# Two decoder layers on one core: u, Toeplitz blocks and halves of q and k moved by transfers instead of part-height ScalarE copies, with a new instruction order and first weights in two parts

## Chip, core and metric

The kernel runs on 1 core of one Trainium2 chip, as one launch. The metric is device microseconds of that core for one execution; smaller is better. Before and after are timed as medians of runs.

## What is computed

Two layers over 512 tokens of width 1024, in float32:

```
for l in range(2):
    h = x @ w_in[l]                       # 1024 -> q | k | v | u, 512 columns each
    attn = diff_attention(q, k, v, ...)   # 4 heads, two score maps of 64 dims each, rotary on q and k, causal
    ssm  = s5_ssm(u, ...)                 # 32 groups of 16 channels, a complex state of 64 each; GELU, GLU (512 x 512)
    mix  = concat(attn, ssm) @ w_out[l]
    x = layer_norm(ALPHA * x + mix)
    x = layer_norm(ALPHA * x + square(relu(x @ w_ff1[l])) @ w_ff2[l])   # 1024 -> 4096 -> 1024
```

## The kernel before

**Products.** Each float32 product is three products of split operands (`mm3`): high x high, high x low, low x high. A weight of 128 x 1024 comes as `raw` by a transfer from SyncE's queue; ScalarE casts it to `whi`; the rest `wlo` is subtracted by VectorE or GpSimd (letters V and P in the plan), or written by ScalarE negated and then completed by an adding transfer that GpSimd issues (A).

**Stages of a layer.** First the "back": projections q, k, v, u of four tiles each, and among them four attention heads in four blocks of 128 tokens and the SSM in four quads (`ssm_pars`, `ssm_outp`, `ssm_a`, `ssm_b`, `ssm_c`), then the four GLU tiles g. Then the mix product with a layer norm, then the feed-forward in eight chunks with a layer norm. In layer 0 the back runs until about 200 us of the profile, in layer 1 from about 550 to 760 us.

**The order.** All instructions are recorded first (`Rec.add`), with a cost each (`Rec.cost`) and a distance between producer and consumer (`Rec.lat`). A list scheduler (`run`) then places them engine by engine, by rank plus an offset per group from the table `pri`, and writes them out in the order of its own clock. So every row of every engine, and SyncE's queue, stands in one planned order; each engine then works through its own rows strictly in turn. Where the planner sees TensorE idle for more than 500 ns, it puts in products of zeros (`wz`, 128 x 256) whose results nobody reads; they keep TensorE occupied. 18 of them stand at the start in any case. I call them fillers.

**Three places with part-height copies.** All of them move rows between partitions:
- `uproj`: a projected tile of u lies in PSUM as 128 channels x 512 tokens, and the SSM wants it as four blocks of 32 partitions by token residue: 16 ScalarE copies of 32 x 128 each, `u<-ps_acc`.
- `ssm_outp`: the Toeplitz block `mx` is filled from `m3` by one full copy and six copies of 32 x 128, `mx<-m`.
- `qkproj`: after the rotary step q is split into high and low, and the halves (64 partitions) are put above each other in two tiles `xq`. For q these are two casts and two subtractions of half height; for k four casts, two subtractions and two memsets of half height into four tiles. The rotary step itself swaps 32-row blocks with four transfers `rt<-rt`.

`cmul` puts its result into `gx` or `hx` with four half-height copies.

**Start.** `start` loads the first two weights (u0 and q0), each in one transfer of 512 KB, one cast and one subtraction of 1024 columns, between eight slices of x.

Of the kernel before, what the change touches and what calls it, by code (L numbers as in the profile page):

```python
# [13 lines left out]
F32 = mybir.dt.float32  # L14
# [32 lines left out]
    "att": [[8, 11, 14, 18], [8, 12, 15, 18]],  # L47
    "s5": [[4, 14], [3, 13]],
# [3 lines left out]
    "eng": {"rope": ["VVV", "VVV"], "tab": ["VVVVVV", "VVVVVV"], "cg": ["VVVV", "VVPV"], "ch": ["VVVV", "VVVV"], "sa": ["PV", "VP"], "sb": ["VVVVVV", "VVVVVV"]},  # L52
    "flo": "AVVV",
    "nlo": "APVAVPPV",
    "glo": "VPPPAPV",
    "seq": "f m1 m7 f m2 m4 f m6 f m5 m3",
    "elo": "VVVV",
    "wb": 4,
    "s5o": "p1 p0 o0 a0 b0 a1 c0 p2 o1 b1 a2 c1 b2 p3 a3 o2 b3 c2 o3 c3",
    "swq": "S",  # L60
    "ao": [-6000, 4000],
    "so": [2000, 19000],
    "ap": [40500, 56750],
    "sp": [31000, 27000],
# [3 lines left out]
    "cuts": [0, 8],  # L68
# [1600 lines left out]
```

## Time and profile before

| | before |
|---|---|
| time, median of 3 runs | 1150.72 us (1150.34 to 1151.69) |
| time of the profiled execution | 1151.48 us |
| its span, first to last instruction | 1149.7 us |
| TensorE busy | 1117.1 us (97%) |
| VectorE busy | 912.5 us (79%) |
| ScalarE busy | 632.2 us (55%) |
| GpSimd busy | 260.3 us (23%) |
| DMA packets | 154.12 MB, mean 134 GB/s |

TensorE's records overlap each other, so its busy share is high even where products start late; and its busy time holds the fillers. Stretches of the span have to be read one by one, since the back of a layer and the feed-forward load the engines differently.

### The profile page before, as it was taken

Reading aid. Unit: us, or ns where it says so; the run is one execution under the profiler, and the core shown is the slowest. Engines: PE = TensorE matmul, PEld = TensorE weight load, DVE = VectorE, ACT = ScalarE, POOL = GpSimd, SP = SyncE. Lnnn points to the kernel's source line nnn. Section 1 sums busy time; section 2 is a strip of 40 time slices with the busy share of each in tenths; the row PEclk is TensorE's granted clock in tenths of the full one; section 3 lists DMA queues with packets and bytes.
Section 4 is the critical chain, followed back from the end, with each engine's and each line's share of the span. In section 5 each row is a group of like instructions: output and inputs, shape, how many; then the busy total and the mean of one; then the engine's idle time right before and its main releaser. Section 6 shows DMA issues by size and latency. Waiting matters only on the chain.

```text
span 1149.7 us, 16190 instructions
## 1 busy us (share of the span) xinstructions
PE 1117.1 (97%) x5840; PEld 936.0 (81%) x5840; DVE 912.5 (79%) x1569; ACT 632.2 (55%) x1202; POOL 260.3 (23%) x198
## 2 busy tenths in 40 slices
PE   9999999999999999999999999999999999999997
PEld 7778877889888888888788878878988888888885
DVE  7898998887778878767792988867777778778788
ACT  7886869425544464444537788873454445445440
POOL 1011110311232242133021221022032143133221
PEclk9999999999999999999999999999999999999999
DMA  9443642441562452553678662652444454355231
GB/s 320 101 119 75 156 121 65 157 135 58 147 155 86 129 168 86 147 147 99 197 202 216 173 169 63 191 155 79 137 139 123 134 128 129 110 147 129 91 110 74
DMA packets 50960, 154.12 MB, mean 134 GB/s; under 512 B 6848, under 2 KB 7104, under 8 KB 50880
## 3 DMA queue, kind: packets, MB, share of 16 engines
q1 hardware_dynamic: 42240, 121.63, 32.6%
q0 software_dynamic: 8640, 31.46, 15.3%
q8 instruction: 46, 0.75, 0.3%
q14 instruction: 34, 0.28, 0.1%
HBM read 110.07 MB, written 7.34 MB: 102 GB/s over the span
## 4 chain that ended last, share of the span: by engine, by line
PE 66%; ACT 5%; DVE 2%; issue 2%; DMA 1%; SPq 0%; DVEq 0%; ACTq 0%; POOLq 0%
PE ps_acc L506 35%; PE ps_sc L506 23%; PE ps_s L506 8%; ACT whi L506 1%; ACT u L506 1%; DVE xq L506 1%; DVE wlo L506 1%; ACT at L506 1%; ACT wlo L506 1%; DMA wlo<-raw 0%; DMA keep<-xq 0%; ACT xq L506 0%; ACT xTh L506 0%; DVE xTl L506 0%; DMA xq<-xs 0%
## 5 line engine op out<-in xcount | busy, mean ns | idle before, releaser
L506 ACT CAST whi<-raw 128x1024 fp32r<-128x1024 f32 x222 | 232.2, 1051 | 264.2 <-PE ps_acc L506 129.4
L506 PE MATMUL ps_acc<-xTh,whi 128*128 128x512 f32 (+1 forms) x712 | 268.9, 379 | 4.6 <-ACT u L506 3.7
L506 PE MATMUL ps_acc<-xTl,whi 128*128 128x512 f32 (+1 forms) x712 | 268.3, 378 | 1.7 <-DVE xTl L506 1.3
L506 PE MATMUL ps_acc<-xTh,wlo 128*128 128x512 f32 (+1 forms) x712 | 268.0, 378 | 0.0
L506 PE MATMUL ps_sc<-whi,slot 128*128 128x512 f32 x784 | 254.5, 391 | 1.2 <-DVE xq L506 0.6
L506 POOL TENSOR_TENSOR wlo<-raw,whi 128x1024 fp32r<-128x1024 f32 x62 | 156.2, 2519 | 418.7 <-ACT whi L506 410.9
L506 PEld LDWEIGHTS ps_sc<-whi,slot 128*128 128x128 f32 x784 | 147.0, 188 | 34.6 <-issue 4.1
L506 DVE TENSOR_TENSOR wlo<-raw,whi 128x1024 fp32r<-128x1024 f32 x100 | 122.0, 1221 | 47.1 <-ACT whi L506 47.0
L506 PEld LDWEIGHTS ps_acc<-xTh,whi 128*128 128x128 f32 x712 | 134.0, 188 | 29.3 <-ACT u L506 4.5
L506 PEld LDWEIGHTS ps_acc<-xTl,whi 128*128 128x128 f32 x712 | 134.1, 188 | 24.7 <-DVE xTl L506 1.9
L506 PE MATMUL ps_sc<-wlo,slot 128*128 128x512 f32 x392 | 153.0, 390 | 0.0
L506 PEld LDWEIGHTS ps_acc<-xTh,wlo 128*128 128x128 f32 x712 | 133.9, 188 | 22.9 <-DMA wlo<-raw 0.3
L506 DVE TENSOR_TENSOR slot<-slot 128x512 fp32r<-128x512 f32 (+4 forms) x143 | 126.5, 893 | 6.5 <-ACT slot L506 6.0
L506 POOL DMA_DIRECT2D wlo<-raw x60 | 53.0, 887 | 231.5 <-ACT wlo L506 114.6
L506 ACT ACTIVATE wlo<-raw 128x1024 fp32r<-128x1024 f32 x60 | 63.4, 1059 | 61.9 <-PE ps_s L506 32.4
L506 PEld LDWEIGHTS ps_sc<-wlo,slot 128*128 128x128 f32 x392 | 73.6, 188 | 14.7
L506 DVE TENSOR_TENSOR xq<-xq,ps_sc 128x512 f32<-128x512 f32 x124 | 83.1, 679 | 0.7 <-PE ps_sc L506 0.7
L506 DVE TENSOR_TENSOR raw<-raw 128x1024 f32<-128x1024 f32 x56 | 68.4, 1221 | 0.6
L506 ACT CAST slot<-slot 128x512 fp32r<-128x512 f32 x56 | 34.5, 617 | 51.1 <-DVE slot L506 49.1
L506 PE MATMUL ps_acc<-whi,xTh 128*128 128x256 f32 (+1 forms) x176 | 56.4, 320 | 0.8 <-ACT u L506 0.7
L506 PE MATMUL ps_acc<-wlo,xTh 128*128 128x256 f32 (+1 forms) x176 | 55.9, 319 | 0.4 <-DVE wlo L506 0.4
L506 PE MATMUL ps_acc<-whi,xTl 128*128 128x256 f32 (+1 forms) x176 | 55.4, 318 | 0.0
(229 smaller groups left out, 1902.3 us busy)
## 6 DMA issues: line engine op xcount, KB each, us to landing
raw<-in_w_ff_dram SPq DMA_DIRECT2D x128, 512.0 KB, 3.5
wlo<-raw POOLq DMA_DIRECT2D x60, 512.0 KB, 5.3
raw<-in_w_qk_dram SPq DMA_DIRECT2D x16, 512.0 KB, 5.2
raw<-in_w_out_dram SPq DMA_DIRECT2D x16, 512.0 KB, 4.1
raw<-in_w_u_dram SPq DMA_DIRECT2D x8, 512.0 KB, 5.4
raw<-in_w_v_dram SPq DMA_DIRECT2D x8, 512.0 KB, 6.6
rt<-rt SPq DMA_DIRECT2D x64, 64.0 KB, 2.6
at<-in_ln_dram SPq DMA_DIRECT2D x16, 256.0 KB, 4.4
```

What stands on the lines that cost most here:

```text
L506: getattr(self.real[op.eng], op.name)(*[_real(x) for x in op.a], **{n: _real(x) for n, x in op.k.items()})
```

## The change

Nothing that is computed changes. What moves data changes in four places, and the order changes everywhere.

- `uproj` (`um` is D in both layers): one ScalarE copy of 128 x 512 from PSUM into a tile `rt`, one transfer of 256 KB to a DRAM tile `ud`, four transfers of 64 KB back into `u`.
- `ssm_outp` (`mm` is D): the six small copies become three transfers of 32, 64 and 96 partitions, `mx<-m3`; the layout of `mx` turns from `[P, 4, P]` to `[P, T, 4, 32]`.
- `qkproj` (`qm` is DD and DA): q in both layers and k in layer 0 are cast and subtracted once at full height; transfers of 64 x 512 then fill `xq`: four for a q, eight for a k. Layer 1's k stays as it was.
- `cmul`: two half-height copies in place of four.
- `start` with cuts 0, 2, 8: each of the first two weights comes as 256 and then 768 columns.
- Planner: part-height operations, accumulating ScalarE operations, float32 products, the products that read `xq`, transfers to fewer than 128 partitions, GpSimd copies and ScalarE's release of a buffer cost more; `att`, `s5`, `s5o`, offsets and `pri` (92 entries before, 117 now, 110 of these new or changed) are other numbers. Which engine makes `wlo` changes for 34 weights: 16 go from VectorE to ScalarE with the adding transfer, 18 from VectorE to GpSimd.

```diff
-    "att": [[8, 11, 14, 18], [8, 12, 15, 18]],
-    "s5": [[4, 14], [3, 13]],
+    "att": [[8, 11, 14, 20], [9, 10, 15, 18]],
+    "s5": [[4, 14], [3, 14]],
...
-    "flo": "AVVV",
+    "flo": "AVPP",
...
-    "glo": "VPPPAPV",
+    "glo": "AVPPAPV",
...
-    "cuts": [0, 8],
+    "cuts": [0, 2, 8],
...
+    "um": ["D", "D"],
+    "qm": ["DD", "DA"],
+    "mm": ["D", "D"],
+    "cc": ["AA", "AA", "AA", "AA"],
...
-            return (650.0 if o.p[1] - o.p[0] == 32 else 475.0) if e == "DMA" else 1030.0, 1550.0 + 1.35 * op.move
+            return (690.0 if o.p[1] - o.p[0] < 128 else 520.0) if e == "DMA" else 1030.0, 1550.0 + 1.35 * op.move
...
+            if r.dt == F32R and r.t.key[1] == "xq":
+                return max(c + {256: 35.0, 384: 50.0, 512: 42.0}.get(o.idx.size, 13.2), 116.0), 0.0
...
+            t += 113.0 * (o.p[1] - o.p[0] < P)
...
+            if PLAN["mm"][l] == "D":
+                Q.dma_start(out=mx[0:(t + 1) * 32, t].rearrange("p a c -> p (a c)"),
+                            in_=m3[(3 - t) * 32:128].rearrange("p a c -> p (a c)"))
+            else:
...
+        if PLAN["qm"][l][z] == "D":
+            A.copy(swp.bitcast(F32R), src)
+            tt(src, swp, SU, src.bitcast(F32R), PLAN["ql"][l][2 * h + z])
+            if z == 0:
+                ta, tb = slot(F32R, "xq"), slot(F32R, "xq")
+                for t_, p, o in ((ta, lo, hi), (tb, hi, lo)):
+                    Q.dma_start(out=t_[p].bitcast(F32), in_=swp[p])
+                    Q.dma_start(out=t_[o].bitcast(F32), in_=src[p])
+                qk_t[l, h, z] = ta, tb
+            else:
+
+                f = [slot(F32R, "xq") for i in range(4)]
+                for i, (w, p) in enumerate(((swp, lo), (swp, hi), (src, lo), (src, hi))):
+                    for o in (lo, hi):
+                        Q.dma_start(out=f[i][o].bitcast(F32), in_=w[p])
+                qk_t[l, h, z] = tuple(f)
...
+        if PLAN["um"][l] == "D":
+
+            w = v4(slot(tag="rt"))
+            A.copy(w, av)
+            d = dram.tile([P, 512], F32, name=f"ud{l}{ct}")
+            Q.dma_start(out=d, in_=w.rearrange("p t n -> p (t n)"))
             for t in range(T):
-                A.copy(u[t * 32:(t + 1) * 32, j, :], av[j * 32:(j + 1) * 32, t, :])
+                Q.dma_start(out=u[t * 32:(t + 1) * 32], in_=d[:, t * P:(t + 1) * P].blocks(4))
```

The order of rows is shown at three places. The first is ScalarE at the very start of the program, before:

```order
L506 CAST whi<-raw 128x1024
L506 CAST xTh<-slot 128x512
L506 CAST whi<-raw 128x1024
L506 CAST xTh<-slot 128x512 x2
L506 ACTIVATE mh<-sm 128x32
```

and now:

```order
L523 CAST whi<-raw 128x256
L523 CAST xTh<-slot 128x512
L523 CAST whi<-raw 128x256
L523 CAST xTh<-slot 128x512
L523 CAST whi<-raw 128x768
L523 CAST xTh<-slot 128x512
```

The casts of the first two weights stand in two pieces, and the second slice of x comes ahead of the larger pieces. In TensorE's rows 18 fillers stand ahead of the first product instead of 30.

The second place is ScalarE behind the second rotary projection of layer 0 (k0), where the first two tiles of u leave PSUM. Before:

```order
L506 ACTIVATE rt<-ps_acc 128x512
L506 ACTIVATE wlo<-raw 128x1024
L506 CAST whi<-raw 128x1024
L506 COPY u<-ps_acc 32x128 x16
L506 CAST xq<-rt 64x512 x2
L506 ACTIVATE wlo<-raw 128x1024
L506 COPY u<-ps_acc 32x128 x16
```

and now:

```order
L523 ACTIVATE rt<-ps_acc 128x512
L523 CAST whi<-raw 128x1024
L523 COPY rt<-ps_acc 128x512
L523 ACTIVATE wlo<-raw 128x1024
L523 CAST whi<-raw 128x1024
L523 CAST rt<-rt 128x512
L523 ACTIVATE wlo<-raw 128x1024
L523 CAST whi<-raw 128x1024
L523 CAST rt<-rt 128x512
L523 COPY rt<-ps_acc 128x512
```

Each row of 16 small copies is one full copy, and the second of these stands behind the casts of q0 and k0 (`CAST rt<-rt`), which wait for the rotary step and its transfers. TensorE's rows hold 53 fillers at this place, ahead of the product that needs the bank which the second copy frees; before, 12 stood a little later.

The third place is SyncE's queue in the same stretch and behind it. Before:

```order
L506 DMA rt<-rt 32x512 x4
L506 DMA raw<-in_w_u_dram 128x1024
L506 DMA dsk<-in_d_s_dram 128x32
L506 DMA gsub<-in_subln_dram 128x2
L506 DMA hb<-in_glu_b_dram 128x8
L506 DMA raw<-in_w_qk_dram 128x1024
L506 DMA raw<-in_w_v_dram 128x1024 x2
```

and now:

```order
L523 DMA xq<-rt 64x512 x8
L523 DMA ud_670<-rt 128x512
L523 DMA ud_675<-rt 128x512
L523 DMA raw<-in_w_qk_dram 128x1024
L523 DMA u<-ud_419 32x4x128 x4
L523 DMA raw<-in_w_v_dram 128x1024 x2
L523 DMA u<-ud_670 32x4x128 x4
L523 DMA u<-ud_675 32x4x128 x4
L523 DMA mx_98<-m_943 32x128
L523 DMA mx_98<-m_943 64x128
L523 DMA mx_98<-m_943 96x128
```

The weight transfers now stand between transfers that wait for computed tiles. SyncE's queue has 466 transfers in all instead of 336. In all of the program 117 fillers stand instead of 168; the products that compute are the same 5,368 before and now.

## Rows read from the trace of the kernel before

**Rows 1.** The page: busy time of each engine, share of the span, instructions.
```profile
PE 1117.1 (97%) x5840; PEld 936.0 (81%) x5840; DVE 912.5 (79%) x1569; ACT 632.2 (55%) x1202; POOL 260.3 (23%) x198
```

**Rows 2.** Windows: stretch, length, busy us (instructions) of PE, PEld, DVE, ACT, POOL.
```profile
25.00:200.00 175.00, 163.79 (x1037) 136.58 (x1037) 158.06 (x422) 136.00 (x363) 23.89 (x35) 0.99 0.43 110
200.00:550.00 350.00, 349.09 (x1659) 292.37 (x1659) 273.25 (x369) 164.63 (x232) 97.47 (x54) 1.00 0.45 127
550.00:760.00 210.00, 201.43 (x1254) 173.25 (x1253) 167.56 (x332) 151.01 (x363) 38.55 (x47) 1.00 0.63 172
760.00:1140.00 380.00, 378.12 (x1779) 314.66 (x1778) 289.65 (x379) 163.77 (x222) 95.62 (x53) 1.00 0.43 119
```

**Rows 3.** The same for the fillers' tile wz alone: PE busy first.
```profile
25.00:200.00 175.00, 15.37 (x127) 12.16 (x127) 0.00 (x0) 0.99 0.43 110
```

**Rows 4.** Waits of PE, 25 to 200 us: for whom, us, times, longest.
```profile
PE ps_s L506 <- ACT mx L506: 2.8, 2, 1.6
PE ps_acc L506 <- ACT u L506: 2.6, 3, 1.4
PE ps_sc L506 <- ACT xq L506: 0.8, 1, 0.8
```

**Rows 5.** Waits of PE, 550 to 760 us.
```profile
PE ps_s L506 <- ACT u L506: 2.0, 3, 1.4
PE ps_acc L506 <- ACT u L506: 1.9, 2, 1.6
```

**Rows 6.** Timeline of PE from 683 us: start, us, what [idle before].
```profile
683.49 0.28 PE L506 MATMUL ps_acc<-whi,xTh 128*128 128x256 f32 x1
685.37 0.50 PE L506 MATMUL ps_acc<-xTh,whi 128*128 128x512 f32 x1 [1.60 <-ACT u L506]
685.71 0.39 PE L506 MATMUL ps_acc<-xTl,whi 128*128 128x512 f32 x1
685.94 0.39 PE L506 MATMUL ps_acc<-xTh,wlo 128*128 128x512 f32 x1
```

**Rows 7.** Timeline of ACT at the same place.
```profile
681.06 4.26 ACT L506 COPY u<-ps_acc 32x128 f32<-32x128 f32 x16
```

**Rows 8.** Groups by shape, ACT and POOL: count | busy us, mean ns | idle before.
```profile
L506 ACT ACTIVATE wlo<-raw 128x1024 fp32r<-128x1024 f32 x60 | 63.4, 1059 | 61.9 <-PE ps_s L506 32.4 <-PE ps_acc L506 17.5 <-issue 9.2
L506 ACT ACTIVATE rt<-ps_acc 128x512 f32<-128x512 f32 x75 | 44.3, 591 | 4.5 <-PE ps_acc L506 4.5
...
L506 ACT CAST xq<-rt 64x512 fp32r<-64x512 f32 x48 | 29.7, 618 | 14.0 <-DVE rt L506 13.2
L506 ACT COPY u<-ps_acc 32x128 f32<-32x128 f32 x112 | 28.7, 256 | 3.0 <-PE ps_acc L506 1.7
...
L506 ACT COPY mx<-m 32x128 f32<-32x128 f32 x48 | 14.2, 296 | 0.6
...
L506 POOL TENSOR_TENSOR wlo<-raw,whi 128x1024 fp32r<-128x1024 f32 x62 | 156.2, 2519 | 418.7 <-ACT whi L506 410.9 <-issue 7.6
```

**Rows 9.** Instructions on tile xq: duration ns min/median/max, first and last start.
```profile
L506 DVE TENSOR_TENSOR xq<-rt,xq x32: 675/686/1690, 30.6 to 744.7; 64x512 fp32r<-64x512 f32 x32
```

**Rows 10.** Tile rt: its transfers, SyncE's time for one, and time to landing.
```profile
L506 SPq DMA_DIRECT2D rt<-rt x64: 507/582/2182, 16.0 to 736.6; - x64
...
DMA to landing us min/median/max: 1.9/2.6/8.6
```

**Rows 11.** The page, transfers: count, KB each, median us to landing.
```profile
keep<-xq SPq DMA_DIRECT2D x12, 256.0 KB, 4.5
slot<-keep SPq DMA_DIRECT2D x12, 256.0 KB, 3.6
```

**Rows 12.** Timeline at the start: PE.
```profile
1.38 5.32 PE L506 MATMUL ps_sc<-wz 128*128 128x256 bf16 x30 [1.38 <-DVE mhalf L506]
6.45 0.47 PE L506 MATMUL ps_acc<-xTh,whi 128*128 128x512 f32 x1
...
7.57 0.48 PE L506 MATMUL ps_acc<-xTl,whi 128*128 128x512 f32 x1
```

More of the change, by code (lines that the diff above doesn't have):

```diff
@@ L51 @@
     "lo": ["AAAVAAPAAAAVAAAAAAAA", "AAAAAAAAAAAAAAAVAAVA"],
-    "eng": {"rope": ["VVV", "VVV"], "tab": ["VVVVVV", "VVVVVV"], "cg": ["VVVV", "VVPV"], "ch": ["VVVV", "VVVV"], "sa": ["PV", "VP"], "sb": ["VVVVVV", "VVVVVV"]},
-    "flo": "AVVV",
+    "eng": {"rope": ["VVV", "VVV"], "tab": ["VVVVVV", "VVVVVV"], "cg": ["VVVV", "VVVV"], "ch": ["VVVV", "VVVV"], "sa": ["PV", "PP"], "sb": ["VVVVVV", "VVVVVV"]},
+    "flo": "AVPP",
     "nlo": "APVAVPPV",
-    "glo": "VPPPAPV",
+    "glo": "AVPPAPV",
     "seq": "f m1 m7 f m2 m4 f m6 f m5 m3",
-    "elo": "VVVV",
+    "elo": "AVVV",
     "wb": 4,
-    "s5o": "p1 p0 o0 a0 b0 a1 c0 p2 o1 b1 a2 c1 b2 p3 a3 o2 b3 c2 o3 c3",
+    "s5o": "p1 p0 o0 a0 b0 c0 o1 a1 p2 b1 a2 b2 c1 p3 a3 o2 b3 c2 o3 c3",
     "swq": "S",
[L61 to L64, printed above, removed]
+    "ao": [-6000, 8000],
+    "so": [2000, 3000],
+    "ap": [56500, 56750],
+    "sp": [33000, 43000],
     "pw": -6000,
@@ L138, in to_broadcast, with blocks @@
         return self._new(("to_broadcast", (shape,), {}), idx=np.broadcast_to(self.idx, shape[1:]))
+    def blocks(self, n):
+        return self._new(("rearrange", ("(j c) n -> c j n",), dict(j=n)))
     def bitcast(self, dt):
@@ L216, in lat @@
         a, b = o.eng, op.eng
+        if a == "ACT" and b == "POOL":
+            return 395.0 if op.name == "dma_start" else 180.0
         if a == b and o.name != "dma_start":
@@ L299, in cost @@
                 n = n * 1.7
-            return 67.0 + n / 0.96, 0.0
+            p = o.p[1] - o.p[0] < P or any(v.t.space != "DRAM" and v.p[1] - v.p[0] < P for _, v in views)
+            return 67.0 + n / 0.96 + 105.0 * p, 0.0
         if e == "ACT":
@@ L306, in cost @@
                 n = n * 2
-            t = (45.0 if s else 90.0) + n / 1.2 + (95.0 if "accum_out" in op.k else 0.0)
+            t = (45.0 if s else 90.0) + n / 1.2 + (130.0 if "accum_out" in op.k else 0.0)
+            t += 113.0 * (o.p[1] - o.p[0] < P)
             return t + 97.0 * any(isinstance(op.k.get(z), View) for z in ("scale", "bias")), 0.0
         if op.name == "memset":
-            return 38.0 + n / 1.2, 0.0
+            return max(170.0, 38.0 + n / 1.2), 0.0
+        if op.name == "tensor_copy":
+            return 50.0 + n / 1.05, 0.0
         return (820.0 + 110.0 * n if op.k.get("op") == ALU.pow else 30.0 + 2.335 * n), 0.0
@@ L420, in run @@
                     break
[L421 removed]
+                start = max(start, rel[v.key][0] + (80.0 if e == "ACT" else 0.0))
             if held is not None:
@@ L888, in cmul @@
             s = slice(g2 * 64, g2 * 64 + 64)
-            o = dst[s].rearrange("p r a (t g c) -> p r a t g c", t=T, g=2)
-            for r in range(2):
-                A.copy(o[:, r, :, :, g2, :], d_[s, :, :, r, :])
+            o = dst[s].rearrange("p r a (t g c) -> p r (a t) g c", t=T, g=2)
+            e = PLAN["cc"][2 * l + (n == T)][g2]
+            (A.copy if e == "A" else (G if e == "P" else V).tensor_copy)(
+                o[:, :, :, g2, :], d_[s].rearrange("p a t r c -> p r (a t) c"))
     def ssm_pars(l, qd, tag="slot"):
@@ L968, in ssm_outp @@
         m3 = pars[l, qd][1]
-        A.copy(mx[:, :, 96:128], m3)
+        A.copy(mx[:, 3], m3)
         for t in range(T - 1):
-            for r in range(t + 1):
-                A.copy(mx[r * 32:(r + 1) * 32, :, t * 32:(t + 1) * 32], m3[(r + 3 - t) * 32:(r + 4 - t) * 32])
+            if PLAN["mm"][l] == "D":
+                Q.dma_start(out=mx[0:(t + 1) * 32, t].rearrange("p a c -> p (a c)"),
+                            in_=m3[(3 - t) * 32:128].rearrange("p a c -> p (a c)"))
+            else:
+                for r in range(t + 1):
+                    A.copy(mx[r * 32:(r + 1) * 32, t], m3[(r + 3 - t) * 32:(r + 4 - t) * 32])
         cmul(l, qd, ct, apr[:, al, 1:], api[:, al, 1:], T, hx, AD, SU)
@@ L1059, in uproj @@
         av = acc.rearrange("p (n t) -> p t n", t=T)
-        for j in range(4):
-            for t in range(T):
-                A.copy(u[t * 32:(t + 1) * 32, j, :], av[j * 32:(j + 1) * 32, t, :])
+        if PLAN["um"][l] == "D":
[3 more added lines that the diff above has]
+            Q.dma_start(out=d, in_=w.rearrange("p t n -> p (t n)"))
+            for t in range(T):
+                Q.dma_start(out=u[t * 32:(t + 1) * 32], in_=d[:, t * P:(t + 1) * P].blocks(4))
+        else:
+            for j in range(4):
+                for t in range(T):
+                    A.copy(u[t * 32:(t + 1) * 32, j, :], av[j * 32:(j + 1) * 32, t, :])
         u_t[l, ct] = u
```

13 lines of the change are left out of this document (6 added, 7 removed).

## Prediction

> **What bounds the kernel now.** I read the page first: TensorE is busy for 97% of the span, the next engine, VectorE, for 79% [rows 1]. So time can only come from where TensorE does not do useful work, and the question is where that is. The windows answer it [rows 2]. In the two long feed-forward stretches TensorE is idle for 350.00 - 349.09 = 0.9 us and 380.00 - 378.12 = 1.9 us; whatever is moved between the other engines there can win 2.8 us at most. In the back of layer 0 (25 to 200 us) it is idle for 175.00 - 163.79 = 11.2 us, and 15.4 us of its busy time are 127 fillers [rows 3], which compute nothing. In the back of layer 1 (550 to 760 us) it is idle for 210.00 - 201.43 = 8.6 us. These three numbers, 35 us together, are what the change can reach, and some more: products follow each other every 0.23 us while each record lasts 0.39 us (685.71 and 685.94 in [rows 6]), so a wait costs its idle time plus 0.16 us. The wait at 683.49 shows it: idle 1.60 us, but 685.37 - 683.49 = 1.88 us lie between two starts of which 0.12 us would do for a product of 256 columns.
>
> Next I asked who ends these waits. In layer 0 it is the small copies into mx (2.8 us, twice) and u (2.6 us, three times) and the half-height casts of q and k (0.8 us, once) [rows 4]; in layer 1 it is the copies into u (2.0 + 1.9 us, five times) [rows 5]. The timeline shows the mechanism: TensorE waits for a bank that ScalarE empties with 16 copies in 4.26 us [rows 6, 7], where a copy of a whole bank takes 0.59 us [rows 8].
>
> In layer 0's back VectorE is nearly full as well, 158.06 of 175 us, ScalarE has 136.00 of 175; in layer 1's back they have 167.56 and 151.01 of 210 [rows 2].
>
> **The change, part by part.**
>
> *ScalarE.* u: 128 copies (112 of them in the row) x 0.256 = 32.8 us go, 8 copies of a bank x 0.59 = 4.7 us come, so -28.1 us. mx: 48 x 0.296 = -14.2 us. q and k: of 48 half-height casts 16 stay (layer 1's k) and 12 of full height come; a half-height cast takes 0.618 us, and full height should take the same, so -20 x 0.618 = -12.4 us [rows 8]. That is 54.7 us less on ScalarE, all of it in the two backs, which hold 287 us of its work. 16 negated copies for `wlo` come instead, 16 x 1.059 = 17 us [rows 8], mostly in the feed-forward, where ScalarE is busy for 165 of 350 us [rows 2].
>
> *The waits on these copies* are the main term: 2.8 + 2.6 + 0.8 + 2.0 + 1.9 = 10.1 us in 11 waits, and 11 x 0.16 = 1.8 us for the restarts: **-11.9 us** if nothing takes their place.
>
> *Fillers.* The order has 84 in layer 0's back behind the first products where 127 were, and 7 in layer 1: 36 fewer. At 15.37 / 127 = 0.121 us each, **-4.4 us** [rows 3]. They moved too: 67 of the 127 stood at the last SSM quads, the end of layer 0's back, which now has 13, while 53 stand behind k0. So the widest planned gap, 53 x 0.121 = 6.4 us, lies there now; it comes ahead of work that VectorE has to get through in any case.
>
> *Start.* The first product starts at 6.45 us, the second only at 7.57 us, behind casts and subtractions of 1024 columns [rows 12]. A quarter of the columns comes first now. The gap between them can close (1.1 us), and the first, after 18 instead of 30 fillers, can come up to half a us sooner. The slices of x still come at the pace of the transfers. I take **-1.2 us**, between 0 and -1.6.
>
> *VectorE.* 12 half-height subtractions fewer x 0.686 = -8.2 us, 5.5 of these in layer 0 [rows 9]. Its 34 `wlo` fewer lie mostly in the feed-forward and win nothing, since TensorE hardly waits there; 18 go to GpSimd at 2.52 us each [rows 8], 45 us more on an engine with 97 of 350 us busy [rows 2]. I cost that at nothing; uncovered it would show as waits on `wlo` in stretches that now lose 2.8 us together, and I allow +2 us.
>
> *Remaining waits.* Of 11.2 + 8.6 = 19.8 us idle, 19.8 - 10.1 = 9.7 us belong to other waits, mostly on ScalarE too. With 55 of its 287 us gone, and a planner that now charges part-height and accumulating operations more, some must go: between 0 and -9.7; I take **-3 us**, nearer to none, since I see no single one of them removed.
>
> *Transfers that come.* SyncE issues 130 more. Its time for a small one is 0.58 us [rows 10], so 75 us in two backs of 385 us: the queue has room. What counts is lateness. A u needs 0.59 + 4.5 + 3.6 = 8.7 us through DRAM, by the nearest transfers of 256 KB [rows 8, 11], instead of 4.1 us (16 x 0.256). In the order, six of the eight u tiles are read back 7 or more us of TensorE's work before their first product; two, in layer 1, only 5 and 2.4 us before. Of the eight sets of Toeplitz transfers seven stand 3 or more us of products ahead of use; in layer 0's first quad the product follows the last of three transfers directly. The halves of k are tight: in each of layer 0's four heads the first score product stands 0.2 to 6 us of products behind the last transfers, typically 2 to 3, and a swap of 64 KB takes 2.6 us in the median to land, 1.9 at least and 8.6 at most [rows 10]. So seven places are exposed. The first quad costs about 2 us in any case, by the quickest landing. At the other six: nothing late, 0; each late by 3 us, +18. I take half a us at each, because most swaps land near the low end: 2 + 3 = **+5 us**.
>
> The Trainium skill speaks of this price (DMA: Bandwidth & Descriptors, "Anatomy of one DMA", measured for transfers that GpSimd issues): about 2.0 us fixed for a transfer, most of it the receipt of the write, plus its bytes over 436 GB/s. By that, as an estimate, a u takes 2 x (2.0 + 0.6) = 5.2 us through DRAM, and the exposed u tiles would hardly be late; the rows say 8.1 us for the same two transfers, in a loaded stretch, and I go by the rows.
>
> Sum: -11.9 - 4.4 - 1.2 - 3 + 5 = -15.5 us. Against the profiled execution, 1151.48 - 15.5 = 1136.0; this execution lies 0.8 us above the median of 1150.72, so the median after should be 1135 us.
>
> **Rivals.**
>
> *Half of it.* Transfers land late by about 2 us at the six places (+12 instead of +3), and the remaining waits stay: -11.9 - 4.4 - 1.2 + 14 = -3.5, or 1147 us. For it: swaps early in layer 0 share the queue with weights, and up to 8.6 us were seen. Against it: ScalarE and VectorE both get lighter.
>
> *Much more.* VectorE is what layer 0's back cannot undercut: 158.06 - 5.5 = 152.6 us instead of 175, so up to 22 us there, and up to 8.6 us in layer 1: -31, or 1120 us. For it: the planner's new distances. Against it: it needs a VectorE that never waits, and 17 us of waiting there now.
>
> *Slower.* One queue, in order: a weight's transfer stands behind transfers that wait for computed tiles, and a read of `ud` behind a write that must have landed. If TensorE waits more than (15.5 + 3) / 6 = 3.1 us at each of the six places, the gain is gone; at 5 us, the time is 1135 - 3 + 30 = 1162. For it: the widest landing times. Against it: most swaps land in 2 to 3 us. The Trainium skill has a rule on this side (the same page, "Bandwidth"): gather transfers to 1 MiB or more, since those under 64 KB are mostly descriptors. The change does the opposite with 64 KB and 128 KB pieces; whether that makes any of them late no row of before shows.
>
> *No change.* What the removed waits give goes into the 53 fillers' gap and into the order's other waits: 1151 us.
>
> **How the numbers follow.** A measurement of this kernel tells about 0.2%, 2.3 us, from no change. Chances: forecast (1128 to 1142) 0.50; half (1142 to 1148.4) 0.18; much more (below 1128) 0.14; no change 0.06; slower 0.12. Faster by over 0.2% is 0.50 + 0.18 + 0.14 = 0.82. The range 1118 to 1150 leaves out the slower case, a part of no change, and the tail below 1118: about 2 in 10.
>
> **What would show it.** Right: no wait of TensorE on copies into u or mx; idle plus fillers of layer 0's back down from 26.6 us to about 17, of layer 1's back from 8.6 to 3 or 4; ScalarE's busy time down by some 40 us (54.7 less, 17 of new negated copies more); the second product within 0.4 us of the first. Wrong: waits of TensorE on `xq<-rt` or `u<-ud` of more than 3 us together, SyncE's queue held by `ud` or `xq` transfers while TensorE waits for `wlo`, or new idle time between 200 and 550 us.

## The result and the profile after

The changed kernel takes 1136.7 us in the median of 4 runs (1131.02 to 1139.96); the kernel before, run beside it, takes 1150.97 us (1150.34 to 1151.69). The ratio is 0.9871, with a 95% interval of 0.9827 to 0.9914: faster, by 14 us. The profiled execution took 1134.67 us, with a span of 1132.9 us where before had 1149.7: 16.8 us less.

The page after, busy time of each engine (PE is TensorE, PEld its weight loads, DVE VectorE, ACT ScalarE, POOL GpSimd; L506, L523 and the like is the line of one helper that issues every instruction) [rows 1]:

```profile
PE 1104.6 (98%) x5789; PEld 928.6 (82%) x5789; DVE 896.7 (79%) x1525; ACT 587.5 (52%) x1000; POOL 316.1 (28%) x224
```

TensorE still bounds the kernel. ScalarE has 632.2 - 587.5 = 44.7 us less to do, GpSimd 316.1 - 260.3 = 55.8 us more. The windows after [rows 2]:

```profile
25.00:200.00 175.00, 165.91 (x1045) 139.06 (x1044) 163.00 (x425) 108.74 (x257) 25.86 (x29) 1.00 0.67 168
200.00:550.00 350.00, 348.48 (x1662) 292.71 (x1661) 274.99 (x363) 170.76 (x230) 120.12 (x66) 1.00 0.52 139
550.00:760.00 210.00, 204.61 (x1283) 176.47 (x1282) 157.36 (x322) 128.21 (x279) 43.08 (x52) 1.00 0.71 195
```

TensorE's idle time in layer 0's back fell from 11.2 to 175.00 - 165.91 = 9.1 us, in layer 1's back from 8.6 to 210.00 - 204.61 = 5.4 us. The fillers after, by the same windows of tile wz alone [rows 3]:

```profile
25.00:200.00 175.00, 10.49 (x84) 7.74 (x84) 0.00 (x0) 1.00 0.67 168
...
550.00:760.00 210.00, 1.11 (x7) 0.52 (x7) 0.00 (x0) 1.00 0.71 195
...
sum 1132.90, PE 16.84 PEld 11.43 DVE 0.17; mean PE 3.37 PEld 2.29 DVE 0.03
```

and their sum over the whole span before:

```profile
sum 1149.70, PE 22.24 PEld 16.87 DVE 0.17; mean PE 4.45 PEld 3.37 DVE 0.03
```

So the 16.8 us of the span can be told apart in three parts. TensorE's idle time went from 1149.7 - 1117.1 = 32.6 to 1132.9 - 1104.6 = 28.3 us: 4.3. Its fillers went from 22.24 to 16.84 us: 5.4. The rest, 7.1 us, is busy time of the useful products, although there are as many as before (5840 - 168 and 5789 - 117, both 5672: the 5,368 that compute and 304 transposes and mask products).

How can the same products be busy for a shorter time? Records of neighbouring products overlap by 0.16 us [rows 6], so a product that comes up to 0.16 us late leaves no idle time at all, and a longer wait loses that much in busy time. A part of what a late operand costs is therefore written down as busy. The feed-forward shows it. Before (busy us, mean ns, then idle time before the group and who ended it):

```profile
L506 PE MATMUL ps_sc<-whi,slot 128*128 128x512 f32 x784 | 254.5, 391 | 1.2 <-DVE xq L506 0.6
```

and after:

```profile
L523 PE MATMUL ps_sc<-whi,slot 128*128 128x512 f32 x784 | 251.6, 390 | 0.2 <-DVE xq L523 0.2
```

Half of these products belong to layer 1. Their first and last start there, before, in run 3 below, in run 6 below, and after:

```profile
L506 PE MATMUL ps_sc<-whi,slot x392: 387/389/472, 836.1 to 1119.0; 128*128 128x512 f32 x196
L515 PE MATMUL ps_sc<-whi,slot x392: 388/389/468, 825.2 to 1108.2; 128*128 128x512 f32 x196
L514 PE MATMUL ps_sc<-whi,slot x392: 387/389/470, 837.2 to 1117.7; 128*128 128x512 f32 x196
L523 PE MATMUL ps_sc<-whi,slot x392: 387/389/471, 821.3 to 1101.8; 128*128 128x512 f32 x196
```

From the first to the last it takes 282.9 us before and 280.5 after: 2.4 us of the gain, of which only 1.0 was idle time (TensorE idle for 1.2 and 0.2 us in these stretches). It is 282.9 to 283.2 us in every run below with the table of before and 280.5 to 281.5 in every run with the new table, whether copies or transfers move the data and whichever costs the planner has. So these 2.4 us belong to the table. The waits that went were on VectorE (`DVE xq`), and the table takes 34 `wlo` from VectorE; that this is the reason was not tried by itself.

A second piece is the clock. Before, a stretch of layer 0's back has half the granted clock (it stands ahead of the last two columns), behind 3.8 us in which TensorE was busy for 2.0:

```profile
155.00:158.80 3.80, 2.04 (x15) 1.61 (x14) 3.71 (x8) 3.67 (x11) 0.00 (x0) 1.00 0.48 184
158.80:162.20 3.40, 3.17 (x14) 2.86 (x14) 1.99 (x7) 3.00 (x12) 1.28 (x1) 0.51 0.00 0
```

After, the windows show no such loss in either back; 3.4 us at half the clock are, as an estimate, 1.7 us of work. The other 4 us of the 7.1 are not located.

Who ends TensorE's waits now, 25 to 200 us [rows 4]:

```profile
PE ps_sc L523 <- DMA xq<-rt: 2.2, 4, 0.9
PE ps_sc L523 <- DVE at L523: 1.8, 1, 1.8
```

and 550 to 760 us [rows 5]:

```profile
PE ps_acc L523 <- DMA wlo<-raw: 1.2, 1, 1.2
...
PE ps_s L523 <- DMA u<-ud: 0.2, 1, 0.2
```

No wait on a copy into u or mx is left. The new transfers are waited for 2.2 + 0.2 = 2.4 us. The start, TensorE's timeline [rows 12]:

```profile
5.09 0.80 PE L523 MATMUL ps_acc<-xTh,whi 128*128 128x512 f32 x2
5.81 0.73 PE L523 MATMUL ps_acc<-xTl,whi 128*128 128x512 f32 x2
...
9.44 0.50 PE L523 MATMUL ps_acc<-xTh,whi 128*128 128x512 f32 x1 [0.53 <-ACT xTh L523]
```

The first product starts 6.45 - 5.09 = 1.36 us earlier and the next follow at once, but TensorE then waits for xTh, the slices of x. The 24th product starts at 13.53 us, where it started at 13.39 before: nothing is left of the lead.

The time after is thus near the forecast. Whether it is so for the forecast's reasons is another question, and most of the runs below go against them.

### The profile page after: what moved, and what is told of

Read it like the earlier page. It is cut to its first block, busy times and chain, and to the rows that moved or that the text cites. A ratio compares the mean times of both kernels' runs of the same rounds, so it can differ in the third digit from the quotient of the medians.

```text
span 1132.9 us, 16111 instructions
## 1 busy us (share of the span) xinstructions
PE 1104.6 (98%) x5789; PEld 928.6 (82%) x5789; DVE 896.7 (79%) x1525; ACT 587.5 (52%) x1000; POOL 316.1 (28%) x224
## 4 chain that ended last, share of the span: by engine, by line
PE 80%; DVE 10%; DMA 4%; ACT 3%; issue 2%; SPq 1%; POOL 0%; DVEq 0%; ACTq 0%; POOLq 0%
PE ps_acc L523 43%; PE ps_sc L523 27%; PE ps_s L523 11%; DVE slot L523 3%; DMA xq<-rt 2%; DVE rt L523 1%; DVE xq L523 1%; SPq L523 1%; DMA xq<-in_x_dram 1%; DMA wlo<-raw 1%; DVE at L523 1%; DVE xTl L523 1%; ACT at L523 1%; DVE wlo L523 1%; ACT whi L523 1%
## 5 line engine op out<-in xcount | busy, mean ns | idle before, releaser
L523 ACT CAST whi<-raw 128x1024 fp32r<-128x1024 f32 (+1 forms) x224 | 232.6, 1042 | 244.7 <-PE ps_acc L523 115.3
L523 POOL TENSOR_TENSOR wlo<-raw,whi 128x1024 fp32r<-128x1024 f32 x80 | 200.4, 2509 | 310.1 <-ACT whi L523 310.1
L523 PE MATMUL ps_acc<-xTh,whi 128*128 128x512 f32 (+1 forms) x712 | 268.9, 380 | 2.7 <-ACT xTh L523 1.6
L523 PE MATMUL ps_acc<-xTl,whi 128*128 128x512 f32 (+1 forms) x712 | 268.2, 379 | 2.0 <-DVE xTl L523 2.0
L523 PE MATMUL ps_acc<-xTh,wlo 128*128 128x512 f32 (+1 forms) x712 | 268.1, 379 | 1.2 <-DMA wlo<-raw 1.2
L523 PE MATMUL ps_sc<-whi,slot 128*128 128x512 f32 x784 | 251.6, 390 | 0.2 <-DVE xq L523 0.2
L523 PEld LDWEIGHTS ps_sc<-whi,slot 128*128 128x128 f32 x784 | 147.1, 188 | 31.4 <-issue 0.6
L523 PEld LDWEIGHTS ps_acc<-xTh,whi 128*128 128x128 f32 x712 | 133.9, 188 | 27.1 <-ACT xTh L523 3.5
L523 PEld LDWEIGHTS ps_acc<-xTl,whi 128*128 128x128 f32 x712 | 133.9, 188 | 25.8 <-DVE xTl L523 3.8
L523 PEld LDWEIGHTS ps_acc<-xTh,wlo 128*128 128x128 f32 x712 | 133.8, 188 | 23.3 <-DMA wlo<-raw 1.3
L523 PE MATMUL ps_sc<-wlo,slot 128*128 128x512 f32 x392 | 152.7, 390 | 0.0
L523 POOL DMA_DIRECT2D wlo<-raw x76 | 67.0, 882 | 261.4 <-ACT wlo L523 153.9
L523 DVE TENSOR_TENSOR slot<-slot 128x512 fp32r<-128x512 f32 (+4 forms) x139 | 118.6, 871 | 8.5 <-ACT slot L523 8.1
L523 ACT ACTIVATE wlo<-raw 128x1024 fp32r<-128x1024 f32 x76 | 80.3, 1059 | 73.4 <-PE ps_s L523 32.8
L523 DVE TENSOR_TENSOR xq<-xq,ps_sc 128x512 f32<-128x512 f32 x124 | 82.5, 679 | 22.3 <-PE ps_sc L523 22.3
L523 DVE TENSOR_TENSOR wlo<-raw,whi 128x1024 fp32r<-128x1024 f32 (+2 forms) x68 | 80.8, 1190 | 19.5 <-ACT whi L523 18.9
L523 PEld LDWEIGHTS ps_sc<-wlo,slot 128*128 128x128 f32 x392 | 73.6, 188 | 15.1
L523 DVE TENSOR_TENSOR raw<-raw 128x1024 f32<-128x1024 f32 x56 | 70.4, 1257 | 18.1 <-POOL wlo L523 14.2
L523 PE MATMUL ps_acc<-whi,xTh 128*128 128x256 f32 (+1 forms) x176 | 56.6, 322 | 0.8 <-ACT xTh L523 0.8
L523 PE MATMUL ps_acc<-whi,xTl 128*128 128x256 f32 (+1 forms) x176 | 56.1, 320 | 0.0
L523 PE MATMUL ps_acc<-wlo,xTh 128*128 128x256 f32 (+1 forms) x176 | 55.3, 316 | 0.9 <-DVE wlo L523 0.9
L523 ACT CAST slot<-slot 128x512 fp32r<-128x512 f32 x56 | 34.6, 619 | 36.6 <-DVE slot L523 33.0
```

The costliest lines, as they stand in the source:

```text
L523: getattr(self.real[op.eng], op.name)(*[_real(x) for x in op.a], **{n: _real(x) for n, x in op.k.items()})
```

## The experiments

Four theories. *Movement theory*, the forecast's: the copies that are gone pay for nearly all, the planner's costs for little. *Costs theory*: the true costs in the planner pay, by an order that has operands ready in time. *Fit theory*: the table of places and offsets was made for these movements and costs, and each is worth what it is worth only with the others. *Clock theory*, formed after the first runs: time is lost to products at 1.2 GHz after gaps, and won back where gaps go. The kernel before was timed beside them: 1151.75 us (19 runs) beside runs 1 to 4, 1151.11 (13) beside runs 5 to 8, 1151.57 (17) beside runs 9 to 12.

**1. The copies back.** The changed kernel with ScalarE's copies:

```
-    "um": ["D", "D"], "qm": ["DD", "DA"], "mm": ["D", "D"],
+    "um": ["A", "A"], "qm": ["AA", "AA"], "mm": ["A", "A"],
```

> The changed kernel with all part-height ScalarE copies back (u, Toeplitz block, halves of q and k) and no transfers for them; tables, costs and start stay as changed. Theory (the copies on ScalarE were the waits): TensorE waits on copies into u and mx return, ScalarE is busy some 50 us more, and the time goes back by about 10 us of the 14 won: 1146 to 1149. Rival (the new tables and costs won it): it stays within 4 us of the changed kernel, 1137 to 1141. Rival (any change of one part spoils a table that was fitted to the whole): slower than the kernel before, over 1155, with new waits that have nothing to do with u or mx.

Measured: 1149.04 us (1148.39 to 1151.7, 10 runs), ratio to before 0.9978 (0.9968 to 0.9987). Of the 14 us, 12 are gone. ScalarE has 643.4 us of work, 55.9 more than in the changed kernel. Of the waits that the theory named, the one on u returns in layer 0's back (none on mx does). In the last 2 us of the long one the granted clock falls to one half, and stays there for 6.8 us:

```profile
PE ps_acc L523 <- ACT u L523: 6.1, 3, 5.7
```

```profile
46.10:52.90 6.80, 3.65 (x14) 2.82 (x15) 6.70 (x20) 6.63 (x19) 0.97 (x2) 0.50 0.63 145
```

By itself that speaks for the movement theory; but the planner made another order for the copies from a table made for transfers, and run 4 shows what that alone can do.

**2. The transfers alone.** The kernel before with the transfers (the branches for "D" of the Toeplitz blocks, the halves and u, as in the diff of the change), its table and costs kept. The new layout of `mx` and `cmul`'s two copies in place of four come with it:

```
+    "um": ["D", "D"], "qm": ["DD", "DA"], "mm": ["D", "D"],
...
```

> The kernel before with its own tables and costs, and only the transfers (u, Toeplitz block, halves of q and k) in place of the copies. Theory: ScalarE some 50 us lighter, no wait on copies into u or mx, 1139 to 1143. Rival (tables and costs): the old order places the consumers too close behind the transfers, waits on transfers take the place of the waits on copies, 1149 to 1156.

Measured: 1152.18 us (1149.57 to 1155.08, 10 runs), ratio 1.0005 (0.9996 to 1.0015): no gain, although ScalarE has 572.4 us of work instead of 632.2 and none of the waits of [rows 4, 5] is left. Waits of TensorE, 25 to 200 us:

```profile
PE ps_sc L514 <- DMA ud<-rt: 3.0, 1, 3.0
PE ps_sc L514 <- DMA xq<-rt: 2.1, 2, 1.1
```

and 550 to 760 us:

```profile
PE ps_sc L514 <- DMA xq<-rt: 3.0, 2, 2.6
PE ps_acc L514 <- ACT rt L514: 2.3, 1, 2.3
```

The transfers are waited for 3.0 + 2.1 + 3.0 = 8.1 us, against 10.1 for the copies; and the longer of these waits cost more than their length. The timeline of TensorE, and then the windows (granted clock ahead of the last two columns), show the first:

```profile
44.34 0.39 PE L514 MATMUL ps_acc<-xTh,whi 128*128 128x512 f32 x1
47.76 0.87 PE L514 MATMUL ps_sc<-xq 128*128 128x128 f32 x3 [3.03 <-DMA ud<-rt]
...
51.20 0.63 PE L514 MATMUL ps_acc<-xTh,whi 128*128 128x512 f32 x1
51.62 0.63 PE L514 MATMUL ps_acc<-xTl,whi 128*128 128x512 f32 x1
```

```profile
44.30:47.20 2.90, 0.43 (x2) 0.01 (x1) 1.30 (x12) 0.00 (x0) 0.00 (x0) 1.00 1.04 219
47.20:54.00 6.80, 6.24 (x22) 5.21 (x23) 4.60 (x17) 1.35 (x5) 0.00 (x0) 0.50 0.56 164
```

The product that waits reads xq; that the wait is put down to the transfer ud<-rt says only that this one, beside it on SyncE's queue, was the last to come by the profile. After 3 us in which TensorE did almost nothing, the granted clock is 0.50 (1.2 GHz) for 6.8 us, and products of 512 columns follow each other every 0.42 us instead of 0.23. The mean granted clock of this run is 0.990; the kernel before has 0.997, so, as an estimate, about 0.007 x 1150 = 8 us more of full-speed work were lost that way. This was no term of the forecast.

**3. The costs alone.** The kernel before, its copies and table kept; only the planner's prices are new (as in the diff of the change, in `lat`, `cost` and the 80 ns in `run`):

```
-            return 67.0 + n / 0.96, 0.0
+            return 67.0 + n / 0.96 + 105.0 * p, 0.0
+            t += 113.0 * (o.p[1] - o.p[0] < P)
...
```

> The kernel before with its tables and copies, and only the planner's new costs and distances. Theory (copies): the waits on u and mx stay in some form, within 3 us of before, 1148 to 1154. Rival (true spacing wins): 1140 to 1145. Rival (a fitted table is spoilt by any change): over 1155.

Measured: 1140.7 us (1139.71 to 1141.53, 4 runs), ratio 0.9904 (0.989 to 0.9919). The work is the same (ScalarE 632.3 us), no datum takes another way, and nearly three quarters of the gain are there. Waits of TensorE, 25 to 200 us, the largest three:

```profile
PE ps_sc L515 <- DVE at L515: 2.8, 3, 2.0
PE ps_s L515 <- ACT mx L515: 1.1, 2, 0.9
PE ps_acc L515 <- ACT rt L515: 1.0, 2, 0.7
```

and 550 to 760 us, the largest:

```profile
PE ps_s L515 <- ACT xq L515: 1.6, 1, 1.6
```

The waits on u, 6.5 us in [rows 4, 5], are gone while the copies into u still take 0.257 us each. The windows:

```profile
25.00:200.00 175.00, 166.32 (x1063) 140.06 (x1062) 161.76 (x416) 138.41 (x366) 26.64 (x36) 0.99 0.46 116
550.00:760.00 210.00, 204.93 (x1282) 177.25 (x1282) 163.39 (x335) 153.73 (x373) 39.65 (x48) 1.00 0.63 170
```

Idle time is 8.7 us in layer 0's back and 5.1 us in layer 1's, as low as in the changed kernel; the fillers of layer 0's back are still 15.91 us (132 of them). Could any new order of this kernel have gained as much? Its offsets were not shaken, so that is not shown; but runs 2, 8 and 11, other edits of kernels with this table, each move the time by 1.3 us or less.

**4. The offsets shaken.** The changed kernel with 1 us added to or taken from every entry of "pri", by turns:

```
-    "pri": {"1a30": [-9000, -12000], "1q1": [18000, 30000], ...
+    "pri": {"1a30": [-10000, -13000], "1q1": [19000, 29000], ...
```

> The changed kernel with every entry of the offset table moved by 1000 up or down, a control: it says how much time a change of the order costs that is about nothing. If the tables are no finer than the rest, it stays within 3 us of the changed kernel, 1134 to 1140; if the gain hangs on the fitted table, it loses 5 us or more, over 1142, and what e1 to e3 lose up to that amount says nothing of their part.

Measured: 1163.95 us (1159.87 to 1167.37, 4 runs), ratio 1.0103 (1.0074 to 1.0133). 27 us are lost by a change that moves no work. So a kernel that is planned anew from a table made for something else can lose more than all that is at stake here, and runs 1, 5, 6 and 7 have to be read with that in mind.

**5. Transfers and costs**, with the table of before: run 2's edit and run 3's together.

> The kernel before with the transfers and the true costs together, but its own table of places and offsets. Movement theory (the forecast's: the removed copies pay 16 us, the costs nothing of their own): near the changed kernel, 1136 to 1139. Costs theory (true costs pay about 10 us, the transfers little): as the costs alone, 1139 to 1142. Fit theory (the table is worth its gain only with the movements and costs that it was made for): a table made for copies is a wrong one here, 1146 to 1156.

Measured: 1139.78 us (1137.9 to 1142.05, 4 runs), ratio 0.9902 (0.9887 to 0.9918): as the costs alone. Layer 0's fillers do fall here, to 10.93 us (94), but the clock is at 0.992 where run 3 had 0.997, and what the one gives the other takes.

**6. The old costs** in the changed kernel: run 3's lines taken back.

> The changed kernel with the old costs and latencies in the planner; table, transfers and first weights as changed. Movement theory: 1136 to 1140, since the copies are still gone. Costs theory: what the costs gave alone is lost, 1145 to 1148. Fit theory: every plan made with other costs than the table's own loses, 1148 to 1165, as the shaken offsets did (1164).

Measured: 1150.83 us (1146.83 to 1154.6, 10 runs), ratio 0.9999 (0.9985 to 1.0012). Transfers, the new table and the new start together give nothing without the costs.

**7. The table alone**: run 1's edit and run 6's together, so that only the table and the first weights in two parts are new.

> The changed kernel with the copies back and the old costs as well: only its table and the first weights in two parts are new. Movement theory: as the kernel before less the start, about 1150. Costs theory: 1149 to 1152, the same. Fit theory: 1153 to 1170, worse than the kernel before, because neither its copies nor its costs are those for which the table was made.

Measured: 1172.38 us (1171.68 to 1173.82, 4 runs), ratio 1.0186 (1.0171 to 1.0202).

With runs 1 to 3, 5 to 7 and the two kernels, all eight combinations have been timed. Medians in us (the new table comes with the first weights in two parts; `cmul`'s two copies in place of four, 6.0 us less of ScalarE's work, come with the transfers in the upper row and stand on both sides in the lower):

```
                   old costs,   old costs,   new costs,   new costs,
                   copies       transfers    copies       transfers
table of before    1151.1       1152.2       1140.7       1139.8
table of after     1172.4       1150.8       1149.0       1136.7
```

The new costs gain in all four pairs: 10, 12, 23 and 14 us. In the lower row a part of that may be a matter of fit, since that kernel loses 27 us by shaken offsets too. The transfers gain nothing with the old table (+1.1, -0.9) and 22 and 12 us with the new one. The new table loses 21 and 8 us with copies and gains 1 and 3 us with transfers.

**8. Costs and first weights**: run 3 with the first weights in two parts.

```
-    "cuts": [0, 8],
+    "cuts": [0, 2, 8],
```

> The kernel before with the true costs and the first weights in two parts; copies and the rest of its table stay. If the parts of the first weights bring what the forecast put on them (1.2 us) and nothing else moves: 1139.5, against 1140.7 for the costs alone. If a small edit to the plan is enough to move it by several us whatever the edit (fit theory): anything from 1136 to 1152, with the second product within 0.5 us of the first all the same.

Measured: 1140.88 us (1139.08 to 1143.77, 4 runs), against 1140.7 of run 3: no gain within the spread of either, although the first product starts at 5.06 us.

**9. The order held, copies in the transfers' places.** The changed kernel is planned as it is, and only when the instructions are issued does a transfer become copies, so that TensorE, VectorE and GpSimd have the very order of the changed kernel:

```
+    def copies(self, op, pairs):
+        self.swap[op] = [("ACT", "copy", p, {}) for p in pairs]
...
         for op in order:
-            getattr(self.real[op.eng], op.name)(...)
+            for e, name, a, k in self.swap.get(op, [(op.eng, op.name, op.a, op.k)]):
+                getattr(self.real[e], name)(...)
```

> The changed kernel with every instruction of TensorE, VectorE and GpSimd in the changed order; only the movement goes back: where a transfer of a Toeplitz block, of a half of q or k, or the first transfer of a u stood, ScalarE does the part-height copies instead (the u copies read the moved sum in SBUF), and SyncE issues none of these. ScalarE has about 45 to 60 us more to do, at places planned without it. Movement theory: the waits and fillers that the transfers took away come back, 13 to 20 us, 1150 to 1157, with waits of TensorE on copies into u, mx or xq of over 8 us together. Fit theory (the kernel with copies planned anew lost 12 us by its other order, not by the copies): 1137 to 1143, with few such waits. If ScalarE's work, unplanned for, comes ever later: 1160 or more.

Measured: 1185.02 us (1184.65 to 1188.18, 4 runs), ratio 1.0296 (1.0283 to 1.0309): 48 us more than the changed kernel. The timeline of ScalarE and then TensorE's next product show the longest wait:

```profile
50.03 9.81 ACT L524 COPY u<-rt 32x128 f32<-32x128 f32 x32
59.87 0.30 ACT L524 COPY idw<-ct 128x128 f32<-128x128 f32 x1
...
61.84 0.60 ACT L524 COPY gx<-slot 64x512 f32<-64x512 f32 x1
```

```profile
63.21 1.30 PE L524 MATMUL ps_s<-idw,gx 128*128 128x144 f32 x4 [9.29 <-ACT gx L524]
```

Two u tiles' copies stand together, 32 copies in 9.81 us; idw and gx, whose work is short, are queued behind them, and TensorE waits 9.3 us for gx. None of the large waits here is on u, mx or q and k: it is ScalarE's other work that comes late (gx 9.3, rt 6.7 us in layer 0's back). The number that both the movement and the fit theory gave was missed; the third case, ScalarE's work coming ever later, is what happened. But ScalarE got more to do than the 45 to 60 us that were reckoned with. It has 679.6 us, 92 more than the changed kernel and 47 more than the kernel before:

```profile
L524 ACT CAST xq<-rt 64x512 fp32r<-64x512 f32 x80 | 49.0, 617 | 8.1 <-DVE rt L524 6.8
L524 ACT COPY u<-rt 32x128 f32<-32x128 f32 x128 | 37.8, 295 | 1.5
```

Here 64 half-height copies into xq come on top of the full-height casts, where the kernel before had 48 half-height casts and none of full height, and the copies into u read SBUF at 0.295 us each instead of PSUM at 0.256. So the 48 us are the price of these copies, at places not planned for them, and not of the copies of before. The granted clock, 0.985, makes about 0.013 x 1185 = 15 us of them, as an estimate.

**10. More fillers**, in the same order on every engine: 33 more, in planned gaps from 0.2 us on and up to the ends of the longer ones.

```
                 n = self.fill(pe_end, t, warm, live, extra)
+                self.fill(pe_end + n, t, True, live, extra, 60.0)
+            elif e == "PE" and t - pe_end > 200.0:
+                self.fill(pe_end, t, True, live, extra, 60.0)
```

> The changed kernel in the same order on every engine, with 33 more filler products, put into gaps of 0.2 to 0.5 us and up to the ends of the longer gaps that the plan sees. Clock theory (part of the changed kernel's time, and its spread from 1131 to 1140, is matmul work at 1.2 GHz after gaps): the granted clock is 0.997 or more in every run, the median 1131 to 1134. Rival (gaps on the chip are not where the plan sees them, so that fillers stand in the way of products): 33 times 0.11 us at the most, 1137 to 1141, the clock as before. No change: 1135 to 1138.

Measured: 1136.82 us (1132.32 to 1146.27, 6 runs), ratio 0.9878 (0.985 to 0.9907): no change. The granted clock of the six runs lies between 0.992 and 0.998, as before the edit. Fillers in the planned gaps cost no time that shows beside this spread (33 x 0.11 = 3.6 us at the most would hardly show) and don't hold the clock, so the clock theory's remedy is refuted; that longer runs have a lower clock is still so (below).

**11. TensorE's costs alone**: of run 3's edit only these.

```
-                return max(c * 4, 213.0) + 5.0, 0.0
+                return max(c * 4, 213.0) + 10.0, 0.0
+            if r.dt == F32R and r.t.key[1] == "xq":
+                return max(c + {256: 35.0, 384: 50.0, 512: 42.0}.get(o.idx.size, 13.2), 116.0), 0.0
```

> The kernel before; of the true costs only TensorE's (5 ns more for each four-pass product, 22 to 37 ns more for each attention product that streams xq). If it was TensorE's spacing that the planner had wrong: 1140 to 1144, most of the 10 us that all costs gave. If it was the part-height operations of ScalarE and VectorE: 1149 to 1152. Fit theory: any small edit moves the plan, 1140 to 1160 without pattern.

Measured: 1152.9 us (1150.88 to 1155.12, 10 runs), ratio 1.0011 (1.0002 to 1.002): no gain. Of layer 1's back, 550 to 760 us:

```profile
PE ps_acc L508 <- ACT u L508: 2.0, 2, 1.6
PE ps_s L508 <- ACT u L508: 1.8, 2, 1.4
```

**12. The part-height costs alone**: of run 3's edit the two lines quoted there and the price of sums taken along.

> The kernel before; of the true costs only those of ScalarE's and VectorE's part-height operations (113 and 105 ns more each) and of sums taken along on ScalarE (35 ns). If these were what the planner had wrong: 1140 to 1144, since the copies then stand where ScalarE can have them done in time. If it was TensorE's spacing: 1149 to 1152. Fit theory: 1140 to 1160 without pattern.

Measured: 1145.84 us (1144.31 to 1148.57, 4 runs), ratio 0.9952 (0.994 to 0.9965): 5.7 us less than before, about half of what all costs give. Waits on u in layer 0's back are no longer among those listed; mx is unchanged:

```profile
PE ps_s L509 <- ACT mx L509: 2.8, 2, 1.6
```

and of layer 1's 3.9 us there is left:

```profile
PE ps_s L509 <- ACT u L509: 0.4, 1, 0.4
```

So it was the half-height and quarter-height operations (and the sums taken along, which were not tried apart from them) that the planner had too cheap, not TensorE's spacing. The other half of the gain needs the remaining costs (SyncE's time for an issue, the distances to GpSimd, the 80 ns, GpSimd's prices), alone or in company; that was not divided further.

## Why the prediction was right in its number, and where its reasons failed

**The bound** was read rightly: TensorE stays the bound, and what was gained is its idle time, its fillers, and products that followed each other faster.

**The waits on the copies, -11.9.** The waits did go. But they are not the transfers' to claim: the true costs alone remove the 6.5 us on u with the copies still there (run 3), the part-height costs alone nearly all of it (run 12), and the transfers alone remove them all and gain nothing (run 2). With the new table they are worth 12 and 22 us, and a wait on u returns without them (run 1), so the term is not empty; it depends on the order, and the forecast gave it a price of its own. A wait in the profile says that an operand came late; whether the operation is too slow or stands in the wrong place it doesn't say. The forecast took the first for granted. This is the step that failed.

**The planner's costs** stood in the sum only within the -3 us for remaining waits. They are the one part that gains in every pair, 10 to 23 us, and the forecast had them as a detail. The remaining waits themselves did not shrink: idle time other than on the removed copies and the new transfers went from 9.7 to 9.1 + 5.4 - 2.4 = 12.1 us over the two backs.

**Fillers, -4.4.** 36 fewer in the two backs as read from the order, and 15 fewer at the start: 5.4 us less busy. Adding 33 back costs nothing that shows (run 10), so a filler's time seems to count only as the mark of a gap. With either the transfers or the costs alone the fillers of layer 0's back stay at 16 us; with both they fall to 11 (run 5).

**Start, -1.2.** Nothing: the lead of 1.36 us is lost to the slices of x by the 24th product, and run 8 confirms it. The forecast had zero as its bound, and named the slices' pace as the reason.

**The transfers' lateness, +5.** 2.4 us of waits, with 0.16 us for each of five restarts 3.2. Slightly under the 3 us that were to mean a failure; in run 10, with the same order, it is 3.4 + 0.5 = 3.9 us. In another order it is more: 8.1 us in run 2, 11.5 + 1.1 = 12.6 in run 4. The two transfers of a u took 4.5 and 3.5 us in the median, as reckoned (4.5 and 3.6). The first quad's Toeplitz product, for which 2 us were set, does not wait.

**What hides in busy time**, +7.1 us of gain, had only 1.8 us in the sum (0.16 for each restart). The feed-forward, thought to be worth 2.8 us at most by the idle time of both layers, gave 2.4 us in layer 1 alone, by the table: that VectorE's 34 fewer `wlo` "win nothing" there is not borne out. The +2 us allowed for `wlo` on GpSimd is not in the forecast's sum; waits on `wlo` in the two backs went from 0.4 to 0.9 + 1.2 = 2.1 us.

**Signs named.** Idle plus fillers fell from 26.6 to 9.1 + 10.5 = 19.6 us in layer 0 (named: 17) and from 8.6 to 5.4 + 1.1 = 6.5 us in layer 1 (named: 3 or 4); ScalarE lost 44.7 us (named: 40; the forecast's own sum is 37.7 and leaves out `cmul`, whose 64 copies of 0.403 us became 32 of 0.618, 6.0 us less); idle time from 200 to 550 us went from 0.9 to 1.5 us. Some 60% of the gain in idle time and fillers that was promised, and the unseen 7.1 us, make a sum that is right by errors that cancel: that it came out so near is luck.

**What copies would cost with the new table** depends on how the order allows for them: 12 us planned anew (run 1), and 48 us when they stand unplanned in the transfers' places and ScalarE has 92 us more to do (run 9). In run 9 the waits are on ScalarE's other work, in run 1 one of 5.7 us is on u itself; so the transfers help there both by freeing ScalarE's queue and by having u in time, and how much each gives is not shown. With the table of before they give nothing (run 2). What is left open: how far 1136.7 us is owed to the movements and how far to the search for the table that fits them. With the table of before, transfers add nothing to the costs (1139.8 and 1140.7); a table made as carefully for copies with the true costs was not tried.

## What to carry to other kernels

Where a planner sets the order, a wait of the bounding engine on a small operation is first a question of place: check what the planner charges for that operation against the trace before moving the work elsewhere. Parts of such a change don't add up; time them in all combinations, and before reading a loss as the price of an edit, shake the plan to see what a new order alone does. And sum gains from busy time of useful products as well as from idle time, since overlapping records hide short waits.

## What the runs showed of the hardware that was not expected

Most kernels with the new transfers vary more from run to run (4 to 14 us from the shortest to the longest run, against 2 to 5 for those with copies), and the longer runs mostly have the lower granted clock: the changed kernel took 1131.0 and 1134.7 us at 0.998 and 1138.7 and 1140.0 us at 0.994 and 0.995; run 10 1132.3 us at 0.998 and 1146.3 us at 0.992; run 5 1137.9 us at 0.994 and 1142.1 us at 0.990. The copies with true costs stay within 1139.7 and 1141.5 us in run 3, within 1139.1 and 1143.8 in run 8. That transfers which land at varying times open gaps after which the clock falls would fit, and run 2's first gap shows one such case; for the longer runs of the changed kernel no trace was taken, so it is not shown for them.

The transfers that were already there mostly got slower beside the new ones. The page after, median us to landing [rows 10, 11]:

```profile
xq<-rt SPq DMA_DIRECT2D x64, 128.0 KB, 4.8
...
rt<-rt SPq DMA_DIRECT2D x64, 64.0 KB, 3.8
```

The 64 KB swaps of q and k took 2.6 us in the median before and take 3.8 now. With the order held and copies in the transfers' places (run 9) they take 2.6 again; in the other four runs with transfers (4, 5, 6 and 10) they take 3.4 to 4.0 us, but in run 2, with the same transfers and the table and costs of before, 2.4. So the transfers alone don't make them slow. Half a tile of q or k takes 4.8 us, longer than either transfer of 256 KB in [rows 11]. The Trainium skill (DMA: Bandwidth & Descriptors, "Anatomy of one DMA", measured for transfers that GpSimd issues: about 2.0 us fixed plus the bytes over 436 GB/s) would give, as an estimate, 2.0 + 0.3 = 2.3 us for 128 KB; half of what was measured in these loaded stretches, and the measurement decides. Its rule to gather transfers (same page, "Bandwidth"), of which the forecast said that no row of before bears on it, is not tested here either: no run gathers the pieces. The 128 KB pieces into xq are waited for 2.1 + 3.0 us in run 2 and 2.2 us in the changed kernel.
